# Rotation by one shuffle, and copies, scalings and modulation evictions on ScalarE or VectorE, whichever the order finds free first

## The chip, the cores and the metric

The kernel runs on one core of a Trainium2 chip, as one program of 43,459 instructions. The metric is the device time of one execution in microseconds (us). Each engine of the core has its own queue and works through it in the order in which the instructions were written: PE (TensorE, matrix products and transposes, results into PSUM), ACT (ScalarE), DVE (VectorE), POOL (GpSimd) and SP, which only issues transfers.

## The reference

The reference is a trunk of two layers over 2048 latent tokens and 256 context tokens of width 1024. What matters here:

```python
for i in range(DEPTH):                                  # two layers
    hl = rms_norm(x, norm_g[i]) * (1.0 + sc_l) + sh_l   # the modulation (hc alike, of the context)
    hc = rms_norm(ctx_h, norm_g[i]) * (1.0 + sc_c) + sh_c
    # layer 0: gated linear attention and a linear recurrence; layer 1: windowed attention and retention
    y_c, y_l = mixer(hc, hl, ...)                       # begins with one projection h @ w_in
    x = x + g_l * (y_l @ w_out)

def apply_rope(x, cos, sin):                            # layer 1, on q, k, rq and rk of the latent tokens
    half = x.shape[-1] // 2                             # heads of 64
    x1, x2 = x[..., :half], x[..., half:]
    return jnp.concatenate([x1 * c - x2 * s, x1 * s + x2 * c], axis=-1)
```

## The kernel before

The tokens come in five pieces, the context (256) and four of 512. Activations lie with features over the partitions. Products in full precision are made from split operands: a weight tile `wr` of 128x512 is rounded to `wh` on ACT (L1085), the rest `wl` = `wr` - `wh` is taken on DVE (L1086), and PE multiplies high by high, high by low and low by high (L1189 in `tm_tiles`, L1211 in `fm_block`). There are 496 such tiles, and five buffers each of `wh` and `wl`.

A piece is normed tile by tile in `norm_piece`: ACT sums the squares (L1316), POOL takes the power (L1299), DVE scales `xt` (L1318), PE transposes four blocks of 128x128 into one PSUM bank (L1363), and the four blocks are evicted with scale and shift into `tm`, on DVE (L1370) or, where the block's number is in `KA[layer]`, on ACT (L1368). `KA = ((), (1, 3))`: in layer 0 DVE takes all four, in layer 1 the engines take turns. Then ACT casts `tm` into the high part of `ya` (L1372) and DVE takes the rest (L1373).

In layer 1 `rope` turns 36 blocks of 128x512 (two heads of 64 features each): POOL multiplies by the cosines (L2049), DVE multiplies four groups of 32 partitions by the sines, each written to the partner group's partitions (L2052), and DVE adds (L2053).

What is written by hand is a recording. `Recorder` hands every instruction with a fixed engine to `Plan.add`, which finds the instructions that it depends on. `Plan.order` then plays the program through with a duration for each kind of instruction (`cost`) and a delay between engines (`wait`), always takes the instruction with the longest chain behind it of those that are ready, and so decides in what order the instructions stand on each engine and which buffer they take. The semaphore waits are put in later, from the order as written, by the framework; they hold whatever the durations turn out to be.

Of the kernel before, what the change touches and what calls it, by code (L numbers as in the profile page):

```python
# [120 lines left out]
class Buffer:  # L121
    def __init__(self, ring, seq, at):
        self.ring, self.seq, self.at = ring, seq, at
        self.spans = Spans(ring.cols * 4)
        self.users = []
        self.slot = self.tile = self.last = None


class Plan:
# [5 lines left out]
    def __init__(self, nc, scratch):  # L135
        self.nc = nc
        self.ops = []
        self.tiles = {}
        self.cells = {}
        self.space = scratch.tile([128, self.WIDE], F32, name="space")  # L140
        self.space_name = self.space.tensor.name
        self.used = 0
        self.starts, self.bufs = [], []
        self.open = None


    def buffer(self, ring):
# [19 lines left out]
    def add(self, eng, fn, args, kw, after=(), line=None):  # L167
        op = len(self.ops)
        deps = {}
        out = kw["out"] if "out" in kw else (args[0] if args and isinstance(args[0], bass.AP) else None)  # L170
        outs = [x for x in (out, kw.get("accum_out")) if x is not None]
        ins = [x for x in (*args, *kw.values()) if isinstance(x, bass.AP) and not any(x is y for y in outs)]
        takes = []
        for x in ins:
            self.touch(x, op, eng, False, deps, takes)
        for x in outs:
            self.touch(x, op, eng, True, deps, takes)
        deps.pop(op, None)
        for o in after:
            if not deps.get(o):  # L180
                deps[o] = False
        self.ops.append((eng, fn, args, kw, line, deps, self.cost(eng, fn.__name__, out, ins, kw), takes))
        return op

    def touch(self, ap, op, eng, write, deps, takes):
        t = ap.tensor
        if type(t).__name__ != "Tile":
            return
        if t._space == MS.DRAM:
            for c in self.dram_cells(ap):  # L190
# [62 lines left out]
    def cost(self, eng, name, out, ins, kw):  # L253
        if name == "preload_act_table_set":
            return 1290.0, 1290.0, 0
        n = 1
# [22 lines left out]
            return t, t + 180.0, WIDE  # L279
        if eng == DVE:  # L280
            kind = PORT if not ps and n > 1 and name not in ("reciprocal", "memset") else 0
            if name == "tensor_tensor_scan":
                t = 66.0 + 2.09 * n
            elif name in ("tensor_scalar", "tensor_copy") and not ps and n > 256:
                t = 66.0 + 60.0 * ptr + 0.525 * n
            elif name == "tensor_tensor_reduce":
                t = 150.0 + 1.045 * n
            elif name == "memset":
                t = 60.0 + 0.26 * n
            else:  # L290
                t = 66.0 + 60.0 * (ptr if name in ("tensor_scalar", "scalar_tensor_tensor") else 0) + 1.045 * n
            return t, t + 86.0, kind
# [15 lines left out]
    def wait(self, j, e):  # L308
# [6 lines left out]
            return lat + SELF.get(e, 0.0) if e in SELF else 0.0  # L315
        return lat + LAT[e]

    def links(self):
        n = len(self.ops)
        succ = [[] for _ in range(n)]  # L320
        for i, o in enumerate(self.ops):
            for j, data in o[5].items():
                d = 0.0 if data is None else self.wait(j, o[0])
                if data is not None and self.ops[j][0] == o[0] and not data:
                    d = 0.0
                succ[j].append((i, d))
        return succ

    @staticmethod
# [29 lines left out]
    def order(self, key):  # L359
# [1 line left out]
        ops, succ = self.ops, self.links()  # L361
        n = len(ops)
        left = [len(o[5]) for o in ops]
        at, start, landed = [0.0] * n, [0.0] * n, [0.0] * n
        self.landed = landed
        done = [False] * n
        later, now = [[] for _ in range(5)], [[] for _ in range(5)]
# [17 lines left out]
                    priors.setdefault(u, []).append(r)  # L385

        def wake(r):
            for k in parked[r]:
                heapq.heappush(later[ops[k][0]], (at[k], k))
            parked[r] = []  # L390

        def hand(r, s, us):
# [27 lines left out]
                        r.free.remove((s, u))  # L420
                        hand(r.gone.pop(id(s)), s, u)

        def place(i, t):

            got = []
            for b in ops[i][7]:
# [3 lines left out]
                for s, us in r.free:  # L430
                    if all(done[u] for u in us) and all(s is not x[1] for x in got):
                        x = 0.0
                        for u in us:
                            d = self.wait(u, ops[i][0])
                            x = max(x, landed[u] + LAT[ops[i][0]] if d is None else start[u] + d)
# [8 lines left out]

        for i in range(n):
            if not left[i]:
                heapq.heappush(later[ops[i][0]], (0.0, i))
        count = 0
        while count < n:
            best = None  # L450
            for e in range(5):
                if now[e]:
# [9 lines left out]
            t, e = best  # L462
            while later[e] and later[e][0][0] <= t:
                i = heapq.heappop(later[e])[1]
                heapq.heappush(now[e], (key[i], i))
# [8 lines left out]
            if ops[i][6][2] == PORT and port > t:  # L474
                free[e] = t
                heapq.heappush(later[e], (port, i))
                continue
            if ops[i][7]:
                got, other = place(i, t)
                if got is None:  # L480
                    free[e] = t
                    if isinstance(other, float):
                        heapq.heappush(later[e], (other, i))
                    else:
                        parked[other].append(i)
# [6 lines left out]
            occ, lat, kind = ops[i][6]  # L492
            if kind == PORT:
                port = t + occ
            elif e == PE and kind != last:
# [4 lines left out]
                elif kind in (SMALL, QUAD):  # L500
                    t += 190.0 if last == WIDE else 90.0
                elif last == TR:
                    t -= min(82.0, max(0.0, t - at[i]))
                last = kind
            start[i], done[i] = t, True
            free[e] = t + occ
# [12 lines left out]
            for k, d in succ[i]:  # L519
                at[k] = max(at[k], landed[i] + LAT[ops[k][0]] if d is None else t + d)  # L520
                left[k] -= 1
                if not left[k]:
                    heapq.heappush(later[ops[k][0]], (at[k], k))
        return start, max(free)


# [244 lines left out]
def host_consts():  # L771
# [20 lines left out]
    c["k_cos"] = np.ascontiguousarray(np.tile(cos.T, (4, 1)))  # L792
    c["k_sin"] = np.ascontiguousarray(np.concatenate([sin.T, -sin.T, sin.T, -sin.T], axis=0))
    i = np.arange(128)
    d = (i[None, :] - i[:, None]).astype(f)
    rel = np.zeros((128, 4, 128), f)
# [28 lines left out]
def trunk_kernel(ctx_: ExitStack, tc: tile.TileContext, I, out: bass.AP):  # L825
# [1218 lines left out]
    def rope(p, raw, dst):  # L2044
# [625 lines left out]
```

## Time and profile before

| | |
|---|---|
| median of 3 runs | 2414.03 us (2407.23 to 2417.83) |
| profiled execution: its time | 2415.39 us |
| profiled execution: its span | 2413.6 us |
| busy PE, DVE, ACT, POOL | 2179.4, 1844.9, 1272.6, 277.6 us |
| mean granted clock of PE | 0.95 |

The span runs from the first to the last instruction; 1.8 us of the execution's time lie outside it. Busy time is time in which an engine has at least one instruction under way. The granted clock is given as a share of full speed.

### The profile page before, as it was taken

How to read it: one execution, taken by the hardware profiler on the slowest of the kernel's cores; microseconds unless marked ns; L12 is line 12 of the kernel's file. 1: busy time of each engine (PE TensorE's matmuls, PEld its weight loads, DVE VectorE, ACT ScalarE, POOL GpSimd, SP SyncE). 2: the span in 40 equal slices, each digit the busy share in tenths (PEclk: the TensorE clock that was granted, in tenths of full speed). 3: DMA queues.
4: the chain of work that ended last, by engine and by line, in shares of the span. 5: the costliest groups of instructions: out<-in, count | busy, mean ns of one | idle time of the engine just before them, and what ended most of it. 6: DMA issues, size and time to landing. Idle time of an engine off the chain costs nothing. (4 is left out here: it accounts for less than half of the span.)

```text
span 2413.6 us, 43459 instructions
## 1 busy us (share of the span) xinstructions
PE 2179.4 (90%) x15721; PEld 1955.4 (81%) x15721; DVE 1844.9 (76%) x3908; ACT 1272.6 (53%) x2721; POOL 277.6 (12%) x350
## 2 busy tenths in 40 slices
PE   6999979879988989788997999979998899899998
PEld 2978768768667978687896889978898798899897
DVE  3667887897899688568776788778887768888786
ACT  2364774655566576354345444465445534566553
POOL 1000110010011000102201122001211000201021
PEclk8999989989989989798998999989999999999999
DMA  8245435544534435764444454425454233526873
GB/s 238 60 115 146 139 91 143 144 144 111 160 109 145 115 86 170 231 187 132 140 121 127 122 150 149 150 76 151 126 162 135 76 89 117 158 79 202 272 242 134
DMA packets 372616, 340.49 MB, mean 141 GB/s; under 512 B 41832, under 2 KB 318768, under 8 KB 372400
## 3 DMA queue, kind: packets, MB, share of 16 engines
q1 hardware_dynamic: 372400, 337.71, 46.8%
q8 instruction: 123, 2.02, 0.3%
q14 instruction: 93, 0.76, 0.1%
HBM read 256.31 MB, written 67.67 MB: 134 GB/s over the span
## 5 line engine op out<-in xcount | busy, mean ns | idle before, releaser
L1211 PE MATMUL psum<-wh,ya 128*128 128x256 f32 x4416 | 858.3, 290 | 13.7 <-ACT wh L1085 4.1
L1211 PEld LDWEIGHTS psum<-wh,ya 128*128 128x128 f32 x4416 | 695.4, 193 | 27.5 <-DVE ya L1373 5.1
L1189 PE MATMUL psum<-ya,wh 128*128 128x256 f32 (+2 forms) x2864 | 687.7, 325 | 23.1 <-DVE tmp L1695 9.3
L1211 PE MATMUL psum<-wl,ya 128*128 128x256 f32 x2208 | 573.6, 289 | 10.7 <-DVE wl L1086 10.7
L1189 PEld LDWEIGHTS psum<-ya,wh 128*128 128x128 f32 (+1 forms) x2864 | 484.2, 192 | 65.8 <-DVE tmp L1695 10.1
L1085 ACT CAST wh<-wr 128x512 fp32r<-128x512 f32 x496 | 303.4, 619 | 358.9 <-PE psum L1189 153.2
L1086 DVE TENSOR_TENSOR wl<-wr,wh 128x512 fp32r<-128x512 f32 x496 | 352.1, 716 | 146.9 <-ACT wh L1085 132.2
L1189 PE MATMUL psum<-ya,wl 128*128 128x256 f32 (+2 forms) x1432 | 450.5, 325 | 5.7 <-DVE wl L1086 4.3
L1211 PEld LDWEIGHTS psum<-wl,ya 128*128 128x128 f32 x2208 | 399.2, 193 | 17.2 <-DVE wl L1086 13.4
L1189 PEld LDWEIGHTS psum<-ya,wl 128*128 128x128 f32 (+1 forms) x1432 | 270.8, 192 | 27.3 <-DVE wl L1086 5.8
L2110 ACT ACTIVATE ub<-ub,s_mx 128x640 f32<-128x640 f32 (+1 forms) x128 | 104.9, 820 | 79.4 <-DVE s_mx L2101 78.4
L2137 ACT CAST ur<-psum 128x512 fp32r<-128x512 f32 (+1 forms) x184 | 93.7, 522 | 93.7 <-PE psum L2135 82.3
L2135 PE MATMUL psum<-c_k_ident,ub 128*128 128x128 f32 x624 | 126.3, 286 | 10.8 <-ACT tm L1368 5.8
L2101 DVE CUSTOM_DVE_ANT_0 ub<-psum,uc 128x640 f32<-128x640 f32 (+2 forms) x128 | 108.4, 847 | 33.5 <-PE psum L2096 30.7
L2138 DVE TENSOR_TENSOR ur<-psum,ur 128x512 fp32r<-128x512 f32 (+1 forms) x184 | 109.3, 605 | 30.7 <-ACT ur L2137 27.9
L2052 DVE TENSOR_TENSOR tmp<-tmp,ub 32x512 f32<-32x512 f32 x144 | 113.2, 786 | 12.4 <-ACT tmp L2328 6.2
L1370 DVE TENSOR_SCALAR tm<-psum,aT,shT 128x128 f32<-128x128 f32 x216 | 78.0, 407 | 38.1 <-PE psum L1363 21.0
L2135 PEld LDWEIGHTS psum<-c_k_ident,ub 128*128 128x128 f32 x624 | 79.0, 145 | 22.7 <-ACT tm L1368 9.3
L2049 POOL TENSOR_TENSOR tmp<-tmp,ub 128x512 f32<-128x512 f32 x20 | 29.7, 1483 | 389.2 <-ACT tmp L2394 217.1
L1299 POOL TENSOR_TENSOR s_rstd<-s_rstd,mhalf 128x1 f32<-128x1 f32 (+2 forms) x88 | 71.1, 810 | 6.8
L1622 ACT ACTIVATE ub<-psum,gb 128x512 f32<-128x512 f32 (+3 forms) x96 | 51.7, 584 | 32.0 <-PE psum L1621 31.7
L2114 DVE TENSOR_SCALAR ub<-ub,s_rs 128x640 f32<-128x640 f32 (+1 forms) x128 | 65.3, 549 | 1.1
(318 smaller groups left out, 3635.9 us busy)
## 6 DMA issues: line engine op xcount, KB each, us to landing
wr<-in_o_w_in_dram SPq DMA_DIRECT2D x192, 256.0 KB, 3.0
wr<-in_e_w_in_dram SPq DMA_DIRECT2D x160, 256.0 KB, 3.1
wr<-in_e_w_out_dram SPq DMA_DIRECT2D x80, 256.0 KB, 3.2
tmp<-gl SPq DMA_DIRECT2D x64, 256.0 KB, 4.1
wr<-in_o_w_out_dram SPq DMA_DIRECT2D x64, 256.0 KB, 3.4
x1l<-tmp SPq DMA_DIRECT2D x40, 256.0 KB, 3.0
xt<-x1l SPq DMA_DIRECT2D x20, 512.0 KB, 4.2
ua<-in_ada_w_dram SPq DMA_DIRECT2D x32, 256.0 KB, 4.3
```

The costliest lines, as they stand in the source:

```text
L1085: S.copy(h[:, 0:n], raw[:, 0:n])
L1086: eng.tensor_tensor(l[:, 0:n], raw[:, 0:n], h.bitcast(F32)[:, 0:n], op=ALU.subtract)
L1189: T.matmul(ps[0:m, q * w:q * w + w], lhsT=a, rhs=b, start=(q == 0 and k == 0 and i == 0), stop=(q == n // w - 1 and k == 7 and i == 2))
L1211: T.matmul(ps, lhsT=a, rhs=b, start=(ti % 2 == 0 and k == 0 and i == 0), stop=((ti % 2 == 1 or ti == len(tiles) - 1) and k == 7 and i == 2))
L1299: G.tensor_tensor(r, r, mhalf[:, 0:n], op=ALU.pow)
L1370: V.tensor_scalar(tm[:, kk], src, sc, sh, op0=ALU.mult, op1=ALU.add)
L2052: V.tensor_tensor(rot.v[to], raw.v[fr], sinb.v[fr], op=ALU.mult)
L2101: V.tensor_tensor_reduce(out=P_[:, c0:c0 + cn], in0=sc[:, so + c0:so + c0 + cn], in1=mask[:, m0:m0 + cn], scale=1.0, scalar=m, op0=ALU.add ...
L2110: tab_act(EXP, out=Ps[h], in_=Ps[h], func=AF.Exp, scale=-1.0, bias=mx[:, h:h + 1], accum_out=sm[:, h:h + 1])
L2135: T.transpose(tr[:, i * 256 + h * 128:i * 256 + h * 128 + 128], Ps[h][:, kb * 128:kb * 128 + 128], ident)
L2137: S.copy(ph[:, 0:n], tr[:, 0:n])
L2138: V.tensor_tensor(pl[:, 0:n], tr[:, 0:n], ph.bitcast(F32)[:, 0:n], op=ALU.subtract)
```

## The change

`rope` now takes one DVE shuffle over all 128 partitions, in which every partition `i` of a group of 32 takes partition `i ^ 16`, then one DVE product with the sines over all 128 partitions, and the sum as before. For that the columns of the layer 1 input weights that make q, k, rq and rk are put in another order on the host (`turned`), so that the two halves of a head lie 16 partitions apart, and the tables of cosines and sines alike.

`Plan.add` makes a second form, on the other of ACT and DVE, of each plain copy, of each scaling, and of each scaling with a shift, unless it is shorter than 64 elements or in BF16. `Plan.order` puts such an instruction up on both engines, and the one that comes to it first takes it. `KA` is `((), ())`: the modulation's evictions are recorded on DVE and may go to ACT. Further, `touch` notes who used each PSUM bank, and makes an instruction depend on the last one that another engine, by the engine first recorded, did on that bank.

```diff
@@ Plan.add @@
+        form = self.other_form(eng, fn.__name__, args, kw)
+        if form:
+            e, fn, args, kw = form
+            self.others[op] = (e, fn, args, kw, line, deps, self.cost(e, fn.__name__, out, ins, kw), takes)
         return op
+
+    def other_form(self, eng, name, args, kw):
+        if eng not in (DVE, ACT):
+            return None
+        if name in ("copy", "tensor_copy") and not kw:
+            out, x = args
+            form = self.copies[ACT + DVE - eng], (out, x), {}
+        elif name == "tensor_scalar" and kw.get("op0") == ALU.mult and kw.get("op1", ALU.add) == ALU.add:
...
+        elif name == "activation" and kw["func"] == AF.Identity and set(kw) == {"out", "in_", "func", "scale", "bias"}:
...
+        elif name == "activation" and kw["func"] == AF.Copy and set(kw) == {"out", "in_", "func", "scale"}:
...
+        if n < 64 or BF16 in (out.dtype, x.dtype) or out.shape != x.shape:
+            return None
+        return (ACT + DVE - eng, *form)
@@ Plan.touch @@
+            if b.ring.psum:
+                hi = max(y for _, y in runs(f0, free)) - 1
+                for k in range(f0 // 512, hi // 512 + 1):
+                    used = b.banks.setdefault(k, {})
+                    for e, o in used.items():
+                        if e != eng and o != op:
+                            deps.setdefault(o, False)
+                    used[eng] = op
@@ Plan.cost, VectorE @@
-            if name == "tensor_tensor_scan":
+            if name == "stream_shuffle":
+                t = 66.0 + 1.17 * n
+            elif name == "tensor_tensor_scan":
@@ Plan.order @@
-        at, start, landed = [0.0] * n, [0.0] * n, [0.0] * n
+        start, landed = [0.0] * n, [0.0] * n
+        at = [{o[0]: 0.0} for o in ops]
+        for i, o in self.others.items():
+            at[i][o[0]] = 0.0
...
+            op = ops[i] if ops[i][0] == e else self.others[i]
...
+            ops[i] = op
@@ -759,13 +826,25 @@
-KA = ((), (1, 3))
+KA = ((), ())
...
+HEAD = np.arange(64).reshape(2, 2, 16).transpose(1, 0, 2).reshape(64)
+
+def turned(w):
+    c = np.arange(w.shape[-1])
+    for a, b in ((0, 640), (1280, 1792)):
+        c[a:b] = c[a:b].reshape(-1, 64)[:, HEAD].reshape(-1)
+    return np.ascontiguousarray(w[..., c])
@@ rope @@
         G.tensor_tensor(dst, raw.v, cosb.v, op=ALU.mult)
-        for a in range(4):
-            to, fr = slice(32 * a, 32 * a + 32), slice(32 * (a ^ 1), 32 * (a ^ 1) + 32)
-            V.tensor_tensor(rot.v[to], raw.v[fr], sinb.v[fr], op=ALU.mult)
+        V.stream_shuffle(rot.v, raw.v, [i ^ 16 for i in range(32)])
+        V.tensor_tensor(rot.v, rot.v, sinb.v, op=ALU.mult)
         V.tensor_tensor(dst, dst, rot.v, op=ALU.add)
```

Since the order is made anew, nearly every place in every queue differs. Over the whole program DVE has 3945 instructions where it had 3910, ACT 2252 where it had 2359; PE, POOL and SP have as many as before. The line numbers of the changed kernel are higher by 78 or 79 in these parts (L1085 is now L1164, L1370 is L1449, L2052 is L2129 and L2130).

The largest movements, counted over the whole order. From DVE to ACT: 69 modulation evictions (L1370, 216 on DVE become 147), 62 scalings of the attention's weights by the row sum (L2114, 128 become 66), 24 scalings of `xt` (L1318, 36 become 12), 50 copies of 64x128 between the states and carries, 12 copies of the modulation's row (L1246) and some 50 others. From ACT to DVE: 96 casts of `wh` (L1085), 40 casts of the turned attention weights (L2137, 184 on ACT become 144), 38 evictions into `ya` (L1846, 68 become 30), 22 casts of `tm` into `ya` (L1372), 18 casts into `ya` of L1862, and some 120 others of 64 to 512 columns.

The first place is the first rotation, on DVE. `tmp` holds the projection and the rotated part, `ub` the sines and the result, `wr`, `wh` and `wl` are weights. Before:

```order
L2052 TENSOR_TENSOR tmp_11090<-tmp_11081,ub 32x512 x2
L1086 TENSOR_TENSOR wl_11112<-wr_11046,wh_11088 128x512
L2052 TENSOR_TENSOR tmp_11090<-tmp_11081,ub 32x512
L1914 SCALAR_TENSOR_TENSOR so_10976<-tmp_11069,lru_hin,so_10976 128x510
L2052 TENSOR_TENSOR tmp_11090<-tmp_11081,ub 32x512
L2204 SCALAR_TENSOR_TENSOR uc<-uc,psum 64x128
L2053 TENSOR_TENSOR ub<-ub,tmp_11090 128x512
```

Now:

```order
L1164 CAST wh_11087<-wr_11050 128x512
L1165 TENSOR_TENSOR wl_11093<-wr_11050,wh_11087 128x512
L2129 STREAM_SHUFFLE tmp_11100<-tmp_11084 128x512
L2282 SCALAR_TENSOR_TENSOR uc<-uc,psum 64x128
L2286 SCALAR_TENSOR_TENSOR uc<-uc,psum 64x128
L2282 SCALAR_TENSOR_TENSOR uc<-uc,psum 64x128
L1980 TENSOR_TENSOR so_10984<-so_10984,psum 128x512
L2130 TENSOR_TENSOR tmp_11100<-tmp_11100,ub 128x512
L2286 SCALAR_TENSOR_TENSOR uc<-uc,psum 64x128
L2131 TENSOR_TENSOR ub<-ub,tmp_11100 128x512
```

Four products over 32 partitions became a shuffle and one product over 128, and just ahead of them DVE casts a weight tile itself and takes the rest of it in the next instruction.

The second place is ACT at the first norm of layer 0. Before, ACT only casts there, and DVE evicts all four blocks of each bank:

```order
L1280 COPY ua_137<-psum 128x512
L1372 CAST ya<-tm_410 128x4x128
L1057 CAST ur<-ua_137 96x512
L1372 CAST ya<-tm_439 128x4x128
L1372 CAST ya<-tm_427 128x4x128
L1372 CAST ya<-tm_475 128x4x128
```

Now:

```order
L1359 COPY ua_137<-psum 128x512
L1449 ACTIVATE tm_411<-psum,shT,aT 128x128 x2
L1451 CAST ya<-tm_411 128x4x128
L1449 ACTIVATE tm_433<-psum,shT,aT 128x128 x2
L1449 ACTIVATE tm_440<-psum,shT,aT 128x128 x2
L1451 CAST ya<-tm_440 128x4x128
L1449 ACTIVATE tm_464<-psum,shT,aT 128x128 x2
```

Two of the four evictions of each of these banks now stand on ACT, and the other two on DVE. Of the 72 banks of the modulation (36 in each layer) 36 were shared so before, all in layer 1; now 60 are shared, 6 are all DVE's and 6 all ACT's. The evictions that hold for the other of the two engines first number 64 on ACT and 28 on DVE before, 83 and 59 now.

The third place is the weights' path in the middle of layer 0, on DVE, as it is now:

```order
L1164 CAST wh_3640<-wr_3581 128x512
L1164 CAST wh_3644<-wr_3589 128x512
L1165 TENSOR_TENSOR wl_3651<-wr_3581,wh_3640 128x512
L1165 TENSOR_TENSOR wl_3660<-wr_3589,wh_3644 128x512
L1834 COPY ua_137<-psum 128x512
```

Here both parts of two weight tiles are made on DVE; before, there was no `wh` cast on this engine.

## Rows read from the trace of the kernel before

**Rows 1.** The page: busy time of each engine and its share.

```profile
PE 2179.4 (90%) x15721; PEld 1955.4 (81%) x15721; DVE 1844.9 (76%) x3908; ACT 1272.6 (53%) x2721; POOL 277.6 (12%) x350
```

**Rows 2.** Busy time by stretch, to 1100 (layer 0) and after; clock, DMA behind.

```profile
0.00:1100.00 1100.00, 960.68 (x6728) 821.71 (x6729) 826.15 (x1767) 620.69 (x1130) 90.94 (x140) 0.92 0.49 141
1100.00:2413.60 1313.60, 1218.75 (x8994) 1133.74 (x8992) 1018.76 (x2141) 651.87 (x1592) 186.68 (x210) 0.97 0.46 141
```

**Rows 3.** Waits of PE on others, whole span: total us, times, longest us.

```profile
PE psum L1363 <- DVE xt L1318: 22.7, 7, 5.9
...
PE psum L1277 <- DMA ua<-in_ada_w_dram: 13.6, 8, 3.1
...
PE psum L1211 <- DVE wl L1086: 10.7, 7, 7.3
PE psum L1619 <- ACT ur L1605: 9.8, 2, 6.9
...
PE psum L1506 <- ACT uc L1491: 6.4, 5, 2.2
PE psum L1619 <- ACT ur L1609: 6.0, 2, 3.4
...
PE psum L2135 <- ACT tm L1368: 5.8, 10, 1.1
PE psum L1189 <- ACT wh L1085: 4.8, 3, 3.4
...
PE psum L1189 <- DVE wl L1086: 4.3, 5, 1.8
PE psum L1211 <- ACT wh L1085: 4.1, 3, 2.0
...
PE psum L1211 <- ACT junk L1832: 0.2, 1, 0.2
PE psum L1620 <- DVE ur L1610: 0.2, 1, 0.2
```

**Rows 4.** Waits of PE from 1100 us on: DVE's first and last row.

```profile
PE psum L1363 <- DVE xt L1318: 19.8, 4, 5.9
...
PE psum L2200 <- DVE uc L2208: 0.3, 1, 0.3
```

**Rows 5.** The rotation's products as a group: busy us, mean ns, idle before.

```profile
L2052 DVE TENSOR_TENSOR tmp<-tmp,ub 32x512 f32<-32x512 f32 x144 | 113.2, 786 | 12.4 <-ACT tmp L2328 6.2 <-ACT ur L2404 1.8 <-ACT tmp L2394 1.0
```

**Rows 6.** The same line by itself: min/median/max ns, first and last start.

```profile
L2052 DVE TENSOR_TENSOR tmp<-tmp,ub x144: 678/684/1765, 1104.1 to 2173.8; 32x512 f32<-32x512 f32 x144
```

**Rows 7.** The first rotation by time: start us, us, idle before in brackets.

```profile
1104.09 2.38 DVE L2052 TENSOR_TENSOR tmp<-tmp,ub 32x512 f32<-32x512 f32 x2 [2.29 <-ACT tmp L2328]
1104.13 1.79 POOL L2049 TENSOR_TENSOR ub<-tmp,ub 128x512 f32<-128x512 f32 x1 [2.28 <-DMA tmp<-gl]
```

**Rows 8.** DVE's groups, shapes apart: busy us, mean ns, idle before.

```profile
L1370 DVE TENSOR_SCALAR tm<-psum,aT,shT 128x128 f32<-128x128 f32 x216 | 78.0, 407 | 38.1 <-PE psum L1363 21.0 <-ACT tm L1368 16.7
L2114 DVE TENSOR_SCALAR ub<-ub,s_rs 128x640 f32<-128x640 f32 x112 | 58.2, 558 | 0.9
...
L1847 DVE SCALAR_TENSOR_TENSOR ya<-psum,gn,ya 128x256 fp32r<-128x256 f32 x68 | 30.7, 480 | 25.0 <-ACT ya L1846 21.6 <-PE psum L1842 3.3
...
L1318 DVE TENSOR_SCALAR xt<-xt,s_rstd 128x1024 f32<-128x1024 f32 x32 | 24.8, 774 | 8.5 <-POOL s_rstd L1299 7.4 <-ACT tm L1368 0.9
...
L1498 DVE COPY ub<-uc 64x128 f32<-64x128 f32 x16 | 3.5, 217 | 2.7 <-PE psum L1545 2.3
...
L1733 DVE CAST ur<-psum 96x512 fp32r<-96x512 f32 x4 | 2.7, 680 | 1.7 <-PE psum L1189 1.7
```

**Rows 9.** Waits of ACT and DVE on each other: total us, times, longest us.

```profile
DVE wl L1086 <- ACT wh L1085: 132.2, 102, 6.1
...
ACT tm L1368 <- DVE tm L1370: 51.1, 40, 5.0
...
DVE tm L1370 <- ACT tm L1368: 16.7, 28, 0.9
```

More of the change, by code (lines that the diff above doesn't have):

```diff
@@ L126, in __init__ @@
         self.slot = self.tile = self.last = None
+        self.banks = {}
 class Plan:
@@ L144, in __init__ @@
         self.open = None
+        self.others = {}
+        self.copies = {ACT: nc.scalar.copy, DVE: nc.vector.tensor_copy}
+        self.act, self.scale = nc.scalar.activation, nc.vector.tensor_scalar
     def buffer(self, ring):
@@ L182, in add @@
         self.ops.append((eng, fn, args, kw, line, deps, self.cost(eng, fn.__name__, out, ins, kw), takes))
-        return op
+        form = self.other_form(eng, fn.__name__, args, kw)
+        if form:
+            e, fn, args, kw = form
+            self.others[op] = (e, fn, args, kw, line, deps, self.cost(e, fn.__name__, out, ins, kw), takes)
+        return op
+    def other_form(self, eng, name, args, kw):
[5 more added lines that the diff above has]
+        elif name == "tensor_scalar" and kw.get("op0") == ALU.mult and kw.get("op1", ALU.add) == ALU.add:
+            out, x, a, b = args
+            if b is None:
+                form = self.act, (), dict(out=out, in_=x, func=AF.Copy, scale=a)
+            elif isinstance(a, float) or isinstance(b, float):
+                return None
+            else:
+                form = self.act, (), dict(out=out, in_=x, func=AF.Identity, scale=a, bias=b)
+        elif name == "activation" and kw["func"] == AF.Identity and set(kw) == {"out", "in_", "func", "scale", "bias"}:
+            out, x = kw["out"], kw["in_"]
+            form = self.scale, (out, x, kw["scale"], kw["bias"]), dict(op0=ALU.mult, op1=ALU.add)
+        elif name == "activation" and kw["func"] == AF.Copy and set(kw) == {"out", "in_", "func", "scale"}:
+            out, x = kw["out"], kw["in_"]
+            form = self.scale, (out, x, kw["scale"], None), dict(op0=ALU.mult)
+        else:
+            return None
+        n = 1
+        for k in out.shape[1:]:
+            n *= k
+        if n < 64 or BF16 in (out.dtype, x.dtype) or out.shape != x.shape:
+            return None
+        return (ACT + DVE - eng, *form)
     def touch(self, ap, op, eng, write, deps, takes):
@@ L316, in wait, with after @@
         return lat + LAT[e]
+    def after(self, j, e, data):
+        if data is None:
+            return 0.0
+        return 0.0 if self.ops[j][0] == e and not data else self.wait(j, e)
     def links(self):
@@ L322, in links @@
             for j, data in o[5].items():
[L323 to L326, printed above, removed]
+                succ[j].append((i, self.after(j, o[0], data)))
         return succ
@@ L363, in order @@
         left = [len(o[5]) for o in ops]
-        at, start, landed = [0.0] * n, [0.0] * n, [0.0] * n
+        start, landed = [0.0] * n, [0.0] * n
+        at = [{o[0]: 0.0} for o in ops]
+        for i, o in self.others.items():
+            at[i][o[0]] = 0.0
+        needs = [[] for _ in range(n)]
+        for i, o in enumerate(ops):
+            for j, data in o[5].items():
+                needs[j].append((i, data))
         self.landed = landed
@@ L387, in wake @@
         def wake(r):
-            for k in parked[r]:
-                heapq.heappush(later[ops[k][0]], (at[k], k))
+            for k, e in parked[r]:
+                heapq.heappush(later[e], (at[k][e], k))
             parked[r] = []
@@ L421, in settle, with place @@
                         hand(r.gone.pop(id(s)), s, u)
-        def place(i, t):
+        def place(i, e, t):
             got = []
@@ L433, in place @@
                         for u in us:
-                            d = self.wait(u, ops[i][0])
-                            x = max(x, landed[u] + LAT[ops[i][0]] if d is None else start[u] + d)
+                            d = self.wait(u, e)
+                            x = max(x, landed[u] + LAT[e] if d is None else start[u] + d)
                         can.append((x, len(can), s, us))
@@ L446, in order @@
             if not left[i]:
-                heapq.heappush(later[ops[i][0]], (0.0, i))
+                for e in at[i]:
+                    heapq.heappush(later[e], (0.0, i))
         count = 0
@@ L451, in order @@
             for e in range(5):
+                for q in (now[e], later[e]):
+                    while q and done[q[0][1]]:
+                        heapq.heappop(q)
                 if now[e]:
@@ L464, in order @@
                 i = heapq.heappop(later[e])[1]
-                heapq.heappush(now[e], (key[i], i))
+                if not done[i]:
+                    heapq.heappush(now[e], (key[i], i))
             i = heapq.heappop(now[e])[1]
@@ L473, in order @@
                     i = same[1]
-            if ops[i][6][2] == PORT and port > t:
+            op = ops[i] if ops[i][0] == e else self.others[i]
+            if op[6][2] == PORT and port > t:
                 free[e] = t
@@ L478, in order @@
             if ops[i][7]:
-                got, other = place(i, t)
+                got, other = place(i, e, t)
                 if got is None:
@@ L484, in order @@
                     else:
-                        parked[other].append(i)
+                        parked[other].append((i, e))
                     continue
@@ L518, in order @@
                     hand(r.gone.pop(id(b.slot), r), b.slot, b.users)
-            for k, d in succ[i]:
-                at[k] = max(at[k], landed[i] + LAT[ops[k][0]] if d is None else t + d)
+            for k, data in needs[i]:
                 left[k] -= 1
-                if not left[k]:
-                    heapq.heappush(later[ops[k][0]], (at[k], k))
+                for f in at[k]:
+                    d = self.after(i, f, data)
+                    at[k][f] = max(at[k][f], landed[i] + LAT[f] if d is None else t + d)
+                    if not left[k]:
+                        heapq.heappush(later[f], (at[k][f], k))
         return start, max(free)
@@ L2662 @@
     vals = {name: np.ascontiguousarray(inputs[name]) for name in _INS}
+    vals["o_w_in"] = turned(vals["o_w_in"])
     vals.update(host_consts())
```

8 lines of the change are left out of this document (4 added, 4 removed).

## The prediction

> **What bounds the kernel now.** I read the page first. PE is busy for 2179.4 us of 2413.6, DVE for 1844.9, ACT for 1272.6 [rows 1]. So PE is the bound over the whole program, and this change gives PE nothing less to do: it can only shorten the 234 us in which PE stands idle, and the time in which it runs at half clock.
>
> Next I read the busy time by stretch. The cut at 1100 us is where layer 1's rotations begin. Before it DVE is busy for 826.2 us of 1100, after it for 1018.8 of 1313.6, and the granted clock is 0.92 and 0.97 [rows 2]. A mean of 0.92 between the two levels of 2.4 and 1.2 GHz means 8% of the full-speed time lost: 88 us before the cut and 39 after, 127 together, at most, because PE also waits during some of it.
>
> Then the waits of PE. DVE ended 34 rows of them, 147.5 us in sum, and ACT 19 rows, 55.2 us; the first and last rows stand in [rows 3]. From 1100 us on DVE's part is 20 rows with 68.3 us [rows 4]. No single wait dominates: the largest row is 22.7 us. The kernel has many small stops, in which one instruction on DVE or ACT comes later than the order had counted on.
>
> To turn a microsecond of wait into time I add its clock. If all lost clock came from waits, it would be 127 / 216.3 (the two sums and 13.6 us of transfers [rows 3]) = 0.59 us for each us; if none did, 0. I take the middle, 0.3, so a us of wait removed gives 1.3.
>
> **The rotation (A).** It removes 144 products over 32 partitions, 113.2 us of DVE [rows 5]. Their median is 684 ns and the longest 1765 [rows 6]: the mean of 786 comes from products that ran beside POOL's product with the cosines, as the two that took 2.38 us while POOL was busy for 1.79 [rows 7]. It adds 36 shuffles and 36 products of 512 columns. The product is 684 ns, since these already took that for 512 columns on 32 partitions. The trace has no shuffle. From below I bound it by a copy (0.43 us, worked out under B), from above by two products (1.37 us); I take one product, 0.684, since it is one pass over 512 elements. Then 113.2 - 36 x 1.368 = 64 us of DVE go away, with the ends 39 and 73. POOL's work stays.
>
> The Trainium skill, page "VectorE: DVE Perf Modes", section on the perf-mode tiers, has a shuffle at about 2,400 ns for 2,048 elements and only at one element a cycle. An estimate from that page alone is 0.8 us for 512, with which 60 us would go away in place of 64. No row here shows a shuffle, and the 4 us would move the sum by less than 1 us.
>
> Less DVE work is not less time by itself. A wait on DVE is an instruction standing behind others, and I let such a queue grow with busy time over idle time. From 1100 us on this is 1018.8 / 294.8 = 3.46. If the 64 us were all, it would be 954.8 / 358.8 = 2.66, 23% less, so 16 us of the 68.3. But the choice (B) puts work back on DVE in layer 1, by my count 47 us more than it takes; counted in full, the ratio is 3.21, 7% less, so 5 us. What is put back was placed where DVE came free first, in gaps, so I count half of it: 11 us, with clock 14. The ends are 5 and 25.
>
> **The choice of engine (B).** What DVE gives up: 69 modulation evictions at 407 ns, 62 scalings at 558, 24 of `xt` at 774, 50 small copies at 217 [rows 8], with the smaller rest (about 33) some 125 us. What it takes: 96 weight casts and about 90 other copies inside SBUF, whose DVE price the trace doesn't show. The scaling of 1024 columns less that of 640 gives 0.56 ns a column, so a copy is 217 + 384 x 0.56 = 432 ns for 512; the upper bound is the cast from PSUM at 680 [rows 8]. I take 0.43, since both sides lie in SBUF as with the scalings. With 40 casts and other evictions out of PSUM at 0.42 to 0.68, and 38 into `ya` at 0.48, DVE takes some 175 us. So DVE gains 50 us of work over the program from the choice, while ACT's count falls by 107 instructions. If the copies cost 0.68, DVE gets 47 us more, which by the share under C costs PE some 7 us.
>
> The gain isn't in these sums but in who is free. Nine waiting rows of PE end with an instruction that may now change sides: 74.6 us in sum [rows 3]. I let each row shrink by the share of its instructions that do: `xt` 24 of 36 of 22.7 us, 15; weights 96 of 496 of 23.9 us, 4.6 (there the high part and the rest then follow each other on DVE, where the rest now waits 132.2 us for ACT in all [rows 9]); `ur` 12 of 40 of 15.8 us, 4.7; the others under 1. That is 25 us, with clock 33. The ends are 0 and 74.6 x 1.59 = 119.
>
> **The added waits (C).** Evictions of one bank by two engines go one after the other: in layer 1 ACT's waited 51.1 us for DVE's and DVE's 16.7 for ACT's [rows 9]. Crossings rise from 92 (64 + 28) to 142 (83 + 59), and at 67.8 / 92 = 0.74 us each that is 37 us more of waiting on ACT and DVE. Behind the waiting eviction stand, on ACT, the cast into `ya` and weight casts; PE waits for both. The new bank entries in the order don't plan for it, since both evictions are recorded on DVE. Of all idle time of ACT and DVE (1709.7 us) PE's waits on them are 202.7, 12%; so 4.4 us reach PE, with clock 6. The ends are 0 and 59 (all of the 37).
>
> Transfers keep their number; their order is made anew with the rest, and I count nothing for it: PE's whole waiting on transfers is 13.6 us, all of it on `ua`, the modulation's weights at the start [rows 3].
>
> **The sum.** It is made against the profiled execution, 2415.4 us, 1.4 above the median of the runs: 2415.4 - 14 - 33 + 6 = 2374 us.
>
> **The rivals.**
>
> *More than that.* The order is one plan, and what comes free on either engine helps all that stands behind it, also waits that end with an instruction which cannot move, like those on the score reduction. For it speaks that the waits are spread over 53 rows; against it that PE is busy for 90% of the span already [rows 1]. A third of the 202.7 us is 68, with clock 88: 2327 us.
>
> *No change.* The new order has stops of its own. Each stop of now is a place where planned durations were wrong, and the durations are as rough as before: the order places every instruction anew and meets them elsewhere. Then A and B (47 us) are given back in waits that no row of now names: 2415 us. That the rotation is cheaper speaks against it, since that much is certain.
>
> *Slower: the shared banks.* The place is ACT's queue at the norms. An eviction on ACT that waits for DVE's in the same bank holds the 400 weight casts left on ACT, and PE stops at `wh`. The price by direction is 51.1 / 40 = 1.28 us for ACT and 16.7 / 28 = 0.6 for DVE: (83 - 64) x 1.28 + (59 - 28) x 0.6 = 43 us more, and with clock 56. If all of it reaches PE and B brings nothing, 2415.4 - 14 + 56 = 2457 us; with half of it, 2429. It decides from 25 of the 56 us on, with B at nothing (2426, the bound of slower below). For it speaks that at least 24 of layer 0's banks become shared, where the clock is lowest [rows 2]; against it that PE's largest wait behind an ACT eviction is 5.8 us with 36 shared banks now [rows 3].
>
> The Trainium skill, page "PSUM — Partial Sum Buffer", section on bank collisions, says that two engines must not touch one bank and quadrant at once, reads against reads too, so that they have to be kept apart by waits. The rows of the handover agree.
>
> *The change does less than it says*: a shuffle of 1.37 us, and copies on DVE at 0.68. The first takes A from 14 to about 9, the second costs 7: 2386 us, so it lies inside my forecast.
>
> **How the numbers follow.** A measurement of this kernel can tell about 0.5%, 12 us, from no change: below 2402 is faster, above 2426 slower. The forecast (2345 to 2402 us) gets 0.43, more than that 0.22, no change 0.17, slower 0.18. So faster has 0.65, same 0.17, slower 0.18. The range reaches from the rival above the forecast, 2325, to half the shared banks' price, 2430; outside it I leave about a tenth on either side. The forecast's own range is 2345 to 2402.
>
> **What would show it.** A: the shuffle at 0.6 to 0.8 us, x36, the product at about 684 ns, no products over 32 partitions, and DVE's busy time after the cut lower by 10 to 25 us. B: PE's wait for `xt` below 10 us, and DVE's wait for ACT's `wh` well under 132. C: the two rows of evictions waiting for each other at about 100 us together. The whole: PE's idle time down by 25 to 35 us and the granted clock at 0.955 to 0.965. I am wrong if PE's waits on ACT grow beyond 80 us, if weight casts on DVE take over 0.6 us, or if the sum of PE's waits stays while the names in it change.

## The result, and the profile after

The changed kernel takes 2382.19 us (median of 4 runs, 2377.44 to 2382.76), where the kernel before took 2415.93 beside it: a ratio of 0.9859 [0.9826, 0.9892], so 34 us faster. The prediction had 2374. The profiled execution took 2382.27 us. The page's first line, the span with its mean granted clock, and the busy time by stretch (columns as in [rows 2]):

```profile
PE 2157.6 (91%) x15721; PEld 1947.2 (82%) x15721; DVE 1827.7 (77%) x3979; ACT 1238.0 (52%) x2614; POOL 271.6 (11%) x350
```

```profile
core 0: 2380.5 us, clock 0.948
```

```profile
0.00:1100.00 1100.00, 961.36 (x6783) 822.65 (x6783) 838.66 (x1794) 619.64 (x1138) 94.91 (x147) 0.92 0.49 143
1100.00:2380.50 1280.50, 1196.27 (x8939) 1124.52 (x8938) 989.02 (x2186) 618.34 (x1477) 176.70 (x204) 0.97 0.47 143
```

Against [rows 1] and [rows 2], the span is 33.1 us shorter. PE's busy time fell by 21.8 us (2179.4 to 2157.6), and its idle time only by 11.3 (234.2 to 222.9). The granted clock did not rise: 0.92 and 0.97 by stretch, as before. The waits of PE, with the rows that answer to [rows 3] and [rows 4]:

```profile
PE psum L1442 <- ACT xt L1397: 27.8, 6, 7.3
PE psum L1290 <- DVE wl L1165: 17.3, 7, 5.3
PE psum L1268 <- DVE tmp L1774: 15.2, 6, 8.6
PE psum L1290 <- DVE tmp L1764: 13.6, 4, 11.2
...
PE psum L1356 <- DMA ua<-in_ada_w_dram: 12.4, 7, 2.9
...
PE psum L1442 <- DVE xt L1397: 2.2, 1, 2.2
...
PE psum L1268 <- ACT wh L1164: 1.1, 1, 1.1
...
PE psum L1290 <- DVE wh L1164: 1.0, 2, 0.6
...
PE psum L1698 <- ACT ur L1688: 0.6, 1, 0.6
PE psum L1699 <- DVE ur L1689: 0.6, 1, 0.6
```

The wait for `ur` at L1698 and L1699 (before, L1619 and L1620) is almost gone: 1.2 us, where it was 16.0. That for `xt` grew from 22.7 to 30.0, now mostly behind ACT. At the two products with weights (L1268, L1290) PE waits 76.6 us for DVE and ACT in all, where it was 51.8: `tmp` of L1764 and L1774 is late there now. Over all rows PE waits 139.2 us for DVE (39 rows) and 56.3 for ACT (21 rows), 195.5 where it was 202.7. Most of the 34 us is not in these names.

The new and the moved operations by line: engine, tile, count, min/median/max ns, first and last start:

```profile
L2129 DVE LOAD_MASK_SELECT tmp<-tmp x36: 4/13/15, 1093.8 to 2136.1; - x36
L2129 DVE STREAM_SHUFFLE tmp<-tmp x36: 721/732/752, 1093.8 to 2136.1; 128x512 f32<-128x512 f32 x36
```

```profile
L2130 DVE TENSOR_TENSOR tmp<-tmp,ub x36: 673/686/1712, 1096.7 to 2136.9; 128x512 f32<-128x512 f32 x36
```

```profile
L1164 DVE CAST wh<-wr x96: 393/426/429, 28.4 to 2352.1; 128x512 fp32r<-128x512 f32 x96
```

```profile
L1397 ACT ACTIVATE xt<-xt,s_rstd x23: 1136/1147/1154, 19.4 to 1850.1; 128x1024 f32<-128x1024 f32 x23
...
L1397 DVE TENSOR_SCALAR xt<-xt,s_rstd x9: 746/747/754, 22.5 to 1859.7; 128x1024 f32<-128x1024 f32 x9
```

The waits of DVE and ACT that answer to [rows 9]:

```profile
DVE wl L1165 <- ACT wh L1164: 121.1, 84, 5.3
DVE tm L1449 <- ACT tm L1449: 54.7, 49, 6.5
```

```profile
ACT tm L1449 <- DVE tm L1449: 26.7, 42, 1.3
```

The evictions of a shared bank wait 81.4 us for each other (67.8 before), now mostly on DVE. DVE's wait for ACT's `wh` fell only from 132.2 to 121.1 us.

### The profile page after: what moved, and what is told of

Read it like the earlier page. It is cut to its first block, busy times and chain, and to the rows that moved or that the text cites. A ratio compares the mean times of both kernels' runs of the same rounds, so it can differ in the third digit from the quotient of the medians.

```text
span 2380.5 us, 43320 instructions
## 1 busy us (share of the span) xinstructions
PE 2157.6 (91%) x15721; PEld 1947.2 (82%) x15721; DVE 1827.7 (77%) x3979; ACT 1238.0 (52%) x2614; POOL 271.6 (11%) x350
## 5 line engine op out<-in xcount | busy, mean ns | idle before, releaser
L1290 PE MATMUL psum<-wh,ya 128*128 128x256 f32 x4416 | 862.2, 290 | 35.8 <-DVE tmp L1764 13.6
L1290 PEld LDWEIGHTS psum<-wh,ya 128*128 128x128 f32 x4416 | 695.7, 193 | 52.3 <-DVE tmp L1764 14.8
L1268 PE MATMUL psum<-ya,wh 128*128 128x256 f32 (+2 forms) x2864 | 686.3, 324 | 24.0 <-DVE tmp L1774 15.2
L1290 PE MATMUL psum<-wl,ya 128*128 128x256 f32 x2208 | 567.4, 289 | 17.3 <-DVE wl L1165 17.3
L1268 PEld LDWEIGHTS psum<-ya,wh 128*128 128x128 f32 (+1 forms) x2864 | 478.8, 190 | 69.1 <-DVE tmp L1774 16.2
L1165 DVE TENSOR_TENSOR wl<-wr,wh 128x512 fp32r<-128x512 f32 x496 | 346.6, 704 | 138.6 <-ACT wh L1164 121.1
L1268 PE MATMUL psum<-ya,wl 128*128 128x256 f32 (+3 forms) x1432 | 442.6, 322 | 0.4 <-DVE lru_cb L1739 0.3
L1164 ACT CAST wh<-wr 128x512 fp32r<-128x512 f32 x400 | 245.7, 618 | 368.3 <-PE psum L1290 172.9
L1290 PEld LDWEIGHTS psum<-wl,ya 128*128 128x128 f32 x2208 | 398.1, 194 | 22.0 <-DVE wl L1165 19.0
L1268 PEld LDWEIGHTS psum<-ya,wl 128*128 128x128 f32 (+1 forms) x1432 | 267.3, 190 | 20.5 <-issue 2.0
L2215 ACT CAST ur<-psum 128x512 fp32r<-128x512 f32 (+1 forms) x144 | 73.1, 514 | 95.3 <-PE psum L2213 84.2
L1449 DVE TENSOR_SCALAR tm<-psum,aT,shT 128x128 f32<-128x128 f32 x147 | 53.8, 405 | 57.7 <-ACT tm L1449 54.7
L1449 ACT ACTIVATE tm<-psum,shT,aT 128x128 f32<-128x128 f32 x141 | 59.4, 457 | 53.3 <-DVE tm L1449 26.7
L1442 PE MATMUL psum<-c_k_ident,xt 128*128 128x128 f32 x256 | 44.9, 311 | 32.1 <-ACT xt L1397 27.8
```

What stands on the lines that cost most here:

```text
L1164: S.copy(h[:, 0:n], raw[:, 0:n])
L1165: eng.tensor_tensor(l[:, 0:n], raw[:, 0:n], h.bitcast(F32)[:, 0:n], op=ALU.subtract)
L1268: T.matmul(ps[0:m, q * w:q * w + w], lhsT=a, rhs=b, start=(q == 0 and k == 0 and i == 0), stop=(q == n // w - 1 and k == 7 and i == 2))
L1290: T.matmul(ps, lhsT=a, rhs=b, start=(ti % 2 == 0 and k == 0 and i == 0), stop=((ti % 2 == 1 or ti == len(tiles) - 1) and k == 7 and i == 2))
L1449: V.tensor_scalar(tm[:, kk], src, sc, sh, op0=ALU.mult, op1=ALU.add)
L2215: S.copy(ph[:, 0:n], tr[:, 0:n])
```

## The experiments

The three parts are called rotation, choice (of the engine) and entries (for the users of a PSUM bank). The theory to test was the prediction's: the choice brings most, the rotation some, the entries nothing. The rivals: the parts only work together; or the gain is luck of one order, since each edit makes all orders anew. Times are medians, each ratio is to the kernel before on the same chip.

**e1: rotation alone.** The shuffle and `turned` stay; the choice and the entries go, and `KA` is as before:

```diff
 def other_form(self, eng, name, args, kw):
-    if eng not in (DVE, ACT):
+    if True:
         return None
@@ touch: the bank entries taken out @@
-KA = ((), ())
+KA = ((), (1, 3))
```

> Only the rotation is changed (shuffle, one product, turned weight columns); no instruction may change sides, no bank entries, the modulation's evictions shared as before. Theory that the rotation's freed DVE work pays in layer 1 (term A): 10 to 16 us below the kernel before, ratio 0.993 to 0.996, with the gain between the first and the last rotation and none before the first. Rival, that any new order moves the time by chance: anything from 12 us below to 12 us above, with a gain or loss also ahead of the first rotation.

Measured: 2408.79 us, 0.9972 [0.9962, 0.9983]: 7 us gained by the ratio (5 by the medians), half of the 14 or less. In the profiled executions the first rotation starts at 1103.2 us, where it was 1104.1, so most of the gain lies behind it, as the theory had it.

**e2: choice and entries**, with the four products of the old rotation (and the tables and weight columns that belong to it; `KA` stays as in the change):

```diff
-        V.stream_shuffle(rot.v, raw.v, [i ^ 16 for i in range(32)])
-        V.tensor_tensor(rot.v, rot.v, sinb.v, op=ALU.mult)
+        for a in range(4):
+            to, fr = slice(32 * a, 32 * a + 32), slice(32 * (a ^ 1), 32 * (a ^ 1) + 32)
+            V.tensor_tensor(rot.v[to], raw.v[fr], sinb.v[fr], op=ALU.mult)
```

> The choice of engine with the bank entries and the modulation open to both, the rotation as before. Theory that the choice pays (terms B and C): 15 to 27 us below the kernel before, ratio 0.989 to 0.994, in both layers. Rival, that the choice only moves the waits to other names: within 7 us of the kernel before.

Measured: 2400.53 us, 0.9949 [0.9934, 0.9964]: 12 us gained, less than the 15 to 27 expected.

**e3: entries alone**: the edits of e1 and e2 together, with the entries kept.

> Only the entries of who used a PSUM bank are added to the order's dependences; engines and rotation as before. My prediction gave this nothing: 0.997 to 1.003. Rival, that the gain comes from an order that knows of the handovers: at least 10 us below the kernel before, ratio 0.996 or less, and DVE and ACT wait less for each other at the evictions of layer 1 than the 67.8 us of before.

Measured: 2402.07 us, 0.9952 [0.9940, 0.9964]. This order with the entries, to which the prediction gave nothing, is 12 us faster, and the choice on top of them (e2) brings no more that can be told. The evictions wait for each other in one row only, half of the 67.8 us of before, as the rival had it:

```profile
ACT tm L1447 <- DVE tm L1449: 33.8, 25, 4.4
```

Whether the gain comes from there or from the entries between PE and the readers, this run doesn't separate; e13 does, for the changed kernel.

**e4: the kernel before, ordered anew.** A planned constant of DVE is changed (below this is called the nudge), nothing else:

```diff
-                t = 66.0 + 2.09 * n
+                t = 67.0 + 2.09 * n
@@ and so in the other lines with this 66.0 @@
```

> The kernel before, with 1 ns more in the planned fixed part of three kinds of VectorE instructions (66 to 67 ns), so that the order is made anew with no part of the change in it. Theory that the parts of the change made the gain: within 5 us of the kernel before, ratio 0.998 to 1.002. Rival, that a new order alone moves the time: 8 us or more to either side, which would make differences of that size between the other runs mean little.

Measured: 2418.55 us, 1.0020 [1.0012, 1.0028]. This order is 5 us worse.

**e5: rotation and entries, no choice** (e1 with the entries kept).

> The change without the choice of engine: rotation by shuffle and bank entries, eviction engines fixed as before. If the parts add up as they measured alone (rotation -7, bank entries -12), it comes to about 2395 us, and what the whole change has beyond that (-13) is the choice, which then is worth something only on top of the other two. If the choice brings nothing in any company, it comes to 2380 to 2385 us, as the whole change. If the two parts help the same waits, 2400 to 2403 us. PE's waits on DVE: about 140 us in each case, since both parts alone had 139.

Measured: 2376.38 us, 0.9845 [0.9831, 0.9858]. Without the choice the kernel is as fast as the whole change, and rotation and entries come to more together (37 us) than the 7 and 12 that they gave alone, each measured with one order. PE waits 123.6 us for DVE, below the expected 140.

**e6: rotation and choice, no entries** (the change less its lines in `touch`).

> The change without the bank entries: rotation and choice. If the entries bring here the 12 us that they brought alone, about 2394 us, and the two rows of evictions that wait for each other's engine rise above the 81 us of the changed kernel. If they do nothing here, since with the choice both evictions of a bank are recorded on DVE and get no entry, 2380 to 2385 us, and these rows stay at 75 to 90 us.

Measured: 2417.33 us, 1.0011 [1.0003, 1.0020]. Nothing is left of the 34 us, a greater loss than either theory had. The rows of evictions are not the reason: they sum to 82.5 us, as in the changed kernel.

**e13: entries between ACT and DVE only**, none between PE and the engine that reads the bank:

```diff
-                        if e != eng and o != op:
+                        if e != eng and o != op and PE not in (e, eng):
                             deps.setdefault(o, False)
```

> The changed kernel with bank entries between ScalarE and VectorE only, none between TensorE and the engine that reads the bank. In the order, PE's rows of the two state products that wait for another engine are 35 and 29 then, as without entries (35 and 36), where they are 21 and 21 in the changed kernel. If the entries gain by letting PE fill a bank before it is read, this run loses the gain: 2405 to 2420 us, and PE's wait at layer 1's state product is again about 7 us (0.7 in the changed kernel). If they gain by the evictions' handover between ScalarE and VectorE, it stays at 2380 to 2388 us.

Measured: 2408.30 us, 0.9980 [0.9967, 0.9994]. Most of the gain is lost, so it hangs on the entries between PE and the reader. One place is the state products, where PE writes several blocks of one bank and another engine reads them one after the other: L1585 in layer 0, read by ACT and DVE from L1587 on, and L2278 in layer 1, read by DVE at L2282. In e13, PE's products by line (count | busy us, mean ns | idle before):

```profile
L1585 PE MATMUL psum<-ua,uc 64*128 64x128 f32 x288 | 31.2, 308 | 5.5 <-ACT uc L1570 3.7 <-DVE ub L1587 0.5 <-DMA wr<-in_e_w_in_dram 0.2
L2278 PE MATMUL psum<-ub,uc 128*128 128x128 f32 x144 | 22.5, 283 | 5.4 <-DVE uc L2282 4.0 <-DVE uc L2269 1.1 <-ACT uc L2380 0.2
```

In the changed kernel:

```profile
L1585 PE MATMUL psum<-ua,uc 64*128 64x128 f32 x288 | 23.5, 295 | 3.5 <-ACT uc L1570 3.2 <-DVE uc L1570 0.3
L2278 PE MATMUL psum<-ub,uc 128*128 128x128 f32 x144 | 21.3, 280 | 0.8 <-DVE tmp L2325 0.7
```

And the view of line L2282, first what DVE waited for, then who waited for it, in e13:

```profile
  PE psum L2278: 15.2, 18
  ACT ua L2147: 1.1, 1
...
who waited for it (us, times):
  PEld psum L2278: 5.5, 8
```

In the changed kernel no state product waits for this line any more (one weight load of another product does, for 0.4 us):

```profile
  PE psum L2278: 11.7, 7
who waited for it (us, times):
  POOL uc L2377: 2.5, 1
...
  PEld psum L1978: 0.4, 1
```

Without the entry the order lets DVE read the first block while PE has the others still to write, and both then stop for each other: DVE 18 times for PE, PE's weight loads 8 times for DVE. With it, PE fills the bank first and the reads follow. Busy and idle, the two rows come to 64.6 us in e13 and 49.1 in the changed kernel: 15.5 us. The profiled executions of the two lie 18 us apart (2400.50 and 2382.27), the medians 26, since e13's was one of its fastest. The kernel before, without entries, stands near e13:

```profile
L1506 PE MATMUL psum<-ua,uc 64*128 64x128 f32 x288 | 30.4, 305 | 7.9 <-ACT uc L1491 6.4
L2200 PE MATMUL psum<-ub,uc 128*128 128x128 f32 x144 | 23.0, 285 | 4.2 <-DVE uc L2204 2.6 <-DVE uc L2191 1.0 <-DVE uc L2208 0.3
```

From there to the changed kernel the two rows lose 16.4 us, of which 8.6 are busy time.

**e12: e6, ordered anew** (e6 with the nudge of e4).

> The change without the bank entries, and with the nudge of one planned constant to 67 ns. If the 35 us between the changed kernel and the one without entries are the entries' doing, 2408 to 2424 us; if they were luck of one order, it lies as often near 2385 to 2400.

Measured: 2410.28 us, 0.9989 [0.9980, 0.9998]. A second order without entries has lost the gain too, so the loss is not the luck of one order.

**e7: the changed kernel, ordered anew** (with the nudge of e4, given to the planned time of the shuffle as well).

> The changed kernel with one planned constant for VectorE at 67 in place of 66 ns, so that the order is made anew with nothing to gain. It sizes the luck of an order around the changed kernel: within 6 us of 2382 (as the same nudge gave +5 on the kernel before) if differences of 15 us and more between the other runs are effects of their edits; 2395 us or more if the changed kernel was a lucky order.

Measured: 2359.78 us, 0.9783 [0.9769, 0.9797]. A nudge with nothing to gain brings 22 us more (18 by the two ratios), so the luck of an order is far above the 6 us that I expected. The changed kernel's own order was a poor one: no other with shuffle and entries is slower.

**e8: the scaling of `xt` held on DVE.**

```diff
-        if n < 64 or BF16 in (out.dtype, x.dtype) or out.shape != x.shape:
+        if n < 64 or n > 1023 or BF16 in (out.dtype, x.dtype) or out.shape != x.shape:
```

> The changed kernel with the scaling of xt held on DVE, nothing else barred. If xt is late because it takes 1147 ns on ACT behind other work there, the two rows of PE's wait for xt fall from 30 us to 22 or less (22.7 before the change), and the time to about 2370 us (8 to 10 us of wait by 1.3). If the norm's start is late whatever engine scales, the rows stay at 25 to 32 us and the time within 5 of 2382. If DVE is the engine that is short of room, 24 scalings of 0.75 us put back on it delay what stands behind: 2388 us or more.

Measured: 2378.31 us, 0.9854 [0.9840, 0.9867]. PE's wait in this run:

```profile
PE psum L1442 <- DVE xt L1397: 28.6, 8, 6.4
```

The slower engine was not the cause: the wait stays whichever engine scales. With the scaling on DVE alone it is 16.4 us in e1 and 22.7 in the kernel before, so its 30.0 us in the change are not far outside what orders differ by.

**e9: an entry for every user of a bank on ACT or DVE**, so that the handover between evictions is planned too.

```diff
-                        if e != eng and o != op:
+                        if o != op and (e != eng or eng in (DVE, ACT)):
                             deps.setdefault(o, False)
```

> The changed kernel with an entry for every bank user of ACT and DVE, also where both evictions of a bank are recorded on DVE, so that the order plans for the handover. Evictions that hold for the other engine's eviction fall from 142 in the order to 26. If 12% of such waiting reaches PE, as the prediction had it, the two rows fall from 81 us to about 15, and the time by 8 us with its clock, by 10: about 2372 us. If the handover is on the path of the norms, most of the 66 us: 2330 us or less. If the waiting costs nothing, since the evicting engine has slack there, 2378 to 2386 us.

Measured: 2361.33 us, 0.9783 [0.9766, 0.9799]. Of the 81.4 us of evictions waiting for each other one row is left:

```profile
ACT tm L1449 <- DVE tm L1449: 4.0, 4, 1.7
```

The gain of 21 us over the changed kernel is no larger than that of e7, where these rows still sum to 76.0 us. So the handover's price can't be told from the luck of the order.

**e10: e9 with the weight casts held on ACT.** A flag around each of the two casts (one is shown) makes `other_form` return nothing:

```diff
-        S.copy(h[:, 0:n], raw[:, 0:n])
+        DBG["fixed"] = True
+        S.copy(h[:, 0:n], raw[:, 0:n])
+        DBG["fixed"] = False
@@ other_form @@
-        if eng not in (DVE, ACT):
+        if eng not in (DVE, ACT) or DBG.get("fixed"):
             return None
```

> The version with an entry for every bank user, and the weight casts held on ACT. If casts on DVE make the weights late, as PE's waits at the two weight products say (77 us in the changed kernel, 52 before), these waits fall back to about 50 us and the time from 2361 to 2345 to 2352. If the casts on DVE help, as the prediction's share of 4.6 us has it, 2367 us. If PE's waits only change their names, 2357 to 2365 us.

Measured: 2356.81 us, 0.9768 [0.9753, 0.9783], the fastest of all, though the 4.5 us below e9 are within the luck. PE waits 58.0 us at the two weight products, where it was 76.6 in the changed kernel; but the nudge alone (e7) brings 56.1, so that the casts on DVE made the weights late is not shown. The largest rows in e10:

```profile
PE psum L1446 <- ACT xt L1401: 23.8, 6, 6.0
PE psum L1628 <- DVE ub L1601: 17.3, 8, 5.9
PE psum L1294 <- DVE wl L1169: 15.4, 7, 8.5
```

Put together, with every order that was run:

| | no entries with PE | entries with PE |
|---|---|---|
| old rotation | 2414 (before), 2419 (e4) | 2402 (e3), 2401 (e2) |
| shuffle, no choice | 2409 (e1) | 2376 (e5) |
| shuffle and choice | 2417 (e6), 2410 (e12), 2408 (e13) | 2382 (the change), 2360 (e7), 2378 (e8), 2361 (e9), 2357 (e10) |

The two rows of the state products divide the traces in the same way. Busy and idle, they come to 63 to 69 us in all six orders without entries with PE (before 65.5, e1 69.4, e4 63.2, e6 66.7, e12 64.0, e13 64.6) and to 47 to 55 in all eight with them (e2 51.5, e3 55.1, the change 49.1, e5 50.3, e7 47.9, e8 47.2, e9 46.6, e10 50.4). On average that is 16 us. The two that lie nearest to each other are e4:

```profile
L1506 PE MATMUL psum<-ua,uc 64*128 64x128 f32 x288 | 30.6, 308 | 5.4 <-ACT uc L1491 3.8
L2200 PE MATMUL psum<-ub,uc 128*128 128x128 f32 x144 | 23.4, 291 | 3.8 <-DVE uc L2204 2.3 <-DVE uc L2191 0.9 <-DVE uc L2208 0.3
```

and e3:

```profile
L1585 PE MATMUL psum<-ua,uc 64*128 64x128 f32 x288 | 24.5, 303 | 6.0 <-ACT uc L1570 6.0
L2279 PE MATMUL psum<-ub,uc 128*128 128x128 f32 x144 | 21.0, 287 | 3.6 <-DVE uc L2270 2.1 <-DVE uc L2287 1.1 <-ACT tmp L2326 0.3
```

## Why the prediction came out, and which steps failed

The time lies 8 us from the forecast, but the sum reached it through the wrong terms, so that the number came out is luck. The steps that failed are B's gain of 33 us and a missing term: the sum has none for the bank entries, of which the prediction says only that they don't plan for the handover between evictions. Its own signs say the same. PE's wait for `xt` is 30.0 us, not below 10, and the sum of PE's waits on DVE and ACT nearly stayed (202.7 to 195.5 us) while the names in it changed, which the prediction had given as a sign of being wrong.

**The bank entries: nothing predicted.** I looked only at the entries between two evictions and saw rightly that both are recorded on DVE. I overlooked that the same lines tie PE's writes to the reads of the same bank. In the table the shuffle's six orders with these entries lie at 2357 to 2382 us and its four without at 2408 to 2417: at least 26 us, more than the 22 us by which a nudge moved an order. With the old rotation the difference is 12 to 18 us, which a nudge could have made too. The state products carry some 16 us of it on average; which waits carry the rest was not found.

**B, the choice: 33 us predicted, none shown.** Without it 2376 us, with it 2382 and, ordered anew, 2360; without entries 2409 against 2417, 2410 and 2408. By single rows, `xt` failed (15 us expected, 7 lost). I let a row shrink by the share of its instructions that may move; e5 and e8 have 27.7 and 28.6 us with all of them on DVE, so what holds the scaling is not the engine. What does was not tested; the engine that scales stands idle for POOL's power (`s_rstd`) ahead of that line, 10.9 us in the kernel before, 18.9 in the change and 13.8 in e8. `wl` and `wh` fell from 23.9 to 19.4, as expected, and `ur` at L1619 from 15.8 to 0.6 where I had 4.7 less. But at the weight products the waits for `tmp` came in their place. That is what the rival of no change said of B: the new order has stops of its own. The casts on DVE cost 0.43, as taken.

**A, the rotation: 14 us predicted, 5 to 7 measured alone.** Its parts were right: the shuffle is 732 ns, the product 686, and DVE gives up 113.2 - 26.5 - 27.9 = 59 us for the predicted 64. The Trainium skill, page "VectorE: DVE Perf Modes", section on the perf-mode tiers, gave 0.8 us by estimate; the trace's 0.732 lies between that and my 0.684. DVE's busy time after the cut fell by 29.7 us, a little more than the 10 to 25 expected. What failed is that the price was made for A by itself. With the entries the kernels with the shuffle are 26 us (e3 to e5) and 18 us (e2 to the change) faster, without them 7, near what a nudge alone does (e4). In both pairs the first rotation starts at nearly the same time (1095.3 and 1095.5 us, 1093.6 and 1093.8), so the difference lies behind it, where the shuffle works. But each is a single order, and a nudge moved one by 22 us: that the two need each other is not shown, and why they should is open.

**C, the shared banks: 6 us lost predicted, not to be told.** The handover waits came to 81 us, not the 100 or so expected. e9 took 77 of them away, and its time equals that of e7, which has them. The rival of slower by shared banks falls: the kernels with 76 us and more of these waits are among the fast ones (e7) and the slow ones (e6). The Trainium skill, page "PSUM — Partial Sum Buffer", section on bank collisions, has a write of TensorE kept apart from a reader in the same bank too. The rows of L2278 and L2282 agree (in e13 each waits for the other, 5.5 and 15.2 us), and that half of the rule, which the prediction left out, was the one that cost.

**The clock factor of 1.3** has no support: the mean granted clock is 0.942 to 0.952 in all profiled executions, 0.950 before and 0.948 in both the change and the fastest but one (e7). The idle time of PE fell by 11 us where I expected 25 to 35. The other 22 us came out of its busy time, which I took as fixed. Since the clock did not rise, the premise that the change can only shorten PE's idle time and its time at half clock failed as well. The rows of the state products lost 8.6 us of busy time, since products that are broken up overlap less; the rest was not traced.

## What to carry to other kernels

Where an order is made by a plan, look for resources for which two engines have to wait for each other and which the plan doesn't know: here the entries for PSUM banks, which the prediction took for a detail, were needed for the gain. Before a difference is credited to one edit of such a kernel, order the same program anew with a planned constant changed by a little, on both sides of the comparison: here that alone moved the time by 5 and by 22 us. A wait need not shrink by the share of its instructions that may go to another engine, as the one for `xt` shows; ask first whether the engine is what makes them late.

## What the hardware showed that was not expected

A shuffle of 128x512 in full precision took 732 ns, little more than a product of the same shape (686), with a mask load of 13 ns before it. A cast of 128x512 inside SBUF took 426 ns on DVE, as estimated, and 620 on ACT. The scaling of 128x1024 by a value per partition took 1147 ns on ACT, 747 on DVE. Products in full precision that are broken up by reads of their own bank keep PE busy longer: the 288 of layer 0's states took 31.2 us so (e13), and 23.5 together (the change). The median of a single one is 272 ns in both, with ends that the profile models; what is lost is the overlap of one with the next.
